# Attention values with 512 moving columns per matmul in a one-core hybrid decoder layer

## The chip, the cores and the metric

The kernel runs on one core of one Trainium2 chip. The metric is the device time of one execution in microseconds, the median of several runs. A profile of one more execution shows what each engine did and when. The engines named below are PE (TensorE, matmuls), PEld (its loading of stationary operands), ACT (ScalarE), DVE (VectorE), POOL (GpSimd) and SP (SyncE, which issues most transfers here).

## The reference

One decoder layer over 512 tokens of width 2048: a mixer whose two halves run side by side (stick-breaking attention with 8 heads of 128, and a gated linear recurrence), then an MLP of width 8192. Both sub-layers are preceded by a norm whose shift and scale come from a conditioning vector `c`. Cut to what matters here:

```python
mod = (c_act @ w_ada[l] + b_ada[l]).reshape(B, N_MOD, D)
sh1, sc1, gt1, sh2, sc2, gt2 = [mod[:, j][:, None, :] for j in range(N_MOD)]

h = rmsnorm(x, g_norm_mix[l]) * (1.0 + sc1) + sh1
proj = jnp.einsum('bsd,de->bse', h, w_in[l])
q, k, v, xr, xg = jnp.split(proj, ...)          # widths 1024 each

o_attn = stick_breaking_attention(to_heads(q), to_heads(k), to_heads(v))
...
y = jnp.einsum('bse,ed->bsd', mixed, w_out[l])
x = x + gt1 * y
h = rmsnorm(x, g_norm_mlp[l]) * (1.0 + sc2) + sh2
hid = jnp.square(jax.nn.relu(jnp.einsum('bsd,df->bsf', h, w_mlp_in[l])))
x = x + gt2 * jnp.einsum('bsf,fd->bsd', hid, w_mlp_out[l])
return rmsnorm(x, g_norm_final)
```

The change concerns `v`, the attention values: `h` (512 tokens x 2048) times a 2048 x 1024 part of `w_in`.

## The kernel before, in words

All activations are kept transposed, feature by token, in 16 blocks of 128 features (`k` from 0 to 15); a block of all 512 tokens is one tile of 128 x 512. Products are computed to nearly full float32 precision by three matmuls: each operand is split into a high part, rounded to the format that PE streams quickly (`F32R`), and a low part, the rest. High x high, high x low and low x high are added up in one PSUM bank.

A matmul has a stationary operand (128 x 128, loaded by PEld) and a moving operand (128 partitions by up to 512 columns), and writes 128 x columns into PSUM. The groups of the profile name the moving operand first: `ps_mm<-a,wh` has a moving `a` tile and a stationary slice of a `wh` tile.

For queries, keys and all later products (`mm3`, L258) the weights are stationary and the 512 tokens move. For the values (`v_mm`, L463) it is the other way about, because attention needs them token by feature: the stationary operand is a block of 128 tokens of `hT[k]` (tiles with the tag `a`), and the weights move (tiles `wh` and `wl`, each 128 x 512, the values' weights of four heads for one `k`). The four banks that a group of values uses are filled over all 16 `k`; then `v_evac` (L474) has ACT copy each bank to a high part and DVE subtract it for the low part, and `vt` records where the values of each head and token block lie.

The stages around the change, in order of time:

- L416: the recurrence's input product over all `k`, with the first half of the modulation rows made beside it.
- L489: for each `k`, queries and keys of heads 0 and 1 (four banks `mm`, twelve matmuls), then values of heads 0 to 3 (banks `z` and `o`). `prep2` (L386) makes `hT[k + 2]` beside it on DVE and ACT, with a modulation row.
- `qk_group(2)` (L746): queries and keys of heads 2 and 3, with the attention of heads 0 and 1 woven in.
- `v_group(4)` (L750): values of heads 4 to 7 in four banks `mm`, with the attention of heads 2 and 3 (`scores`, `shares`, `values`) and modulation rows (`adas`, L696, whose passes over `w_ada` are L211) woven in. Its last two `k` are done bank by bank in `ending` (L305), so that each bank is evacuated as it is finished.
- `qk_group(4)` and `qk_group(6)`, with the gates of the recurrence (L569, moving tiles `x`) and attention, the gate branch, the output product, and from L1080 the MLP by Strassen's scheme in steps of 256 columns (L1099 to L1101).

What is woven in comes in `Lane`s (L269): generators whose pieces are written into the program between the main matmuls at a set pace (`tick`). The whole program is then put into an order for each engine by a list scheduler, which takes the ready instruction of the highest priority, judged by its own model of times. Priority is the position in the program; `tc.high_priority(offset=n)` moves it `n` instructions ahead. Weights (`weights`, L230: a transfer on SP into `wr`, a high part by ACT into `wh`, a low part by DVE into `wl`) have an offset of `URGENT` = 150, evacuations one of `EVAC` = 88. There are four `wr` and three each of `wh` and `wl`.

Of the kernel before, what the change touches and what calls it, by code (L numbers as in the profile page):

```python
# [12 lines left out]
AF = mybir.ActivationFunctionType  # L13
ALU = mybir.AluOpType
PSUM = bass.MemoryType.PSUM

P = 128
S = 512
D = 2048
NK = D // P  # L20
# [44 lines left out]
def hybrid_layer_kernel(  # L65
# [32 lines left out]
    def T(tag, dt=F32, cols=None):  # L98
        return new(next(split_tag) if tag == "w4" else tag, dt, cols)
# [13 lines left out]
    act = nc.scalar.activation  # L113
    stt = nc.vector.scalar_tensor_tensor
    tt = nc.vector.tensor_tensor
    mm = nc.tensor.matmul

    def f32(ap):
        return ap.bitcast(F32)
# [110 lines left out]
    def weights(src, tag=None, urgent=URGENT, pin=False):  # L230

        n = src.shape[-1] if len(src.shape) == 2 else src.shape[1] * src.shape[2]
        with tc.high_priority(offset=urgent):
            r = T("wr" if tag not in ("w3", "w4", "ts") else "raw")
            dst = r[:, :n] if len(src.shape) == 2 else r[:, :n].rearrange("p (a b) -> p a b", b=src.shape[2])
            dma = nc.sync.dma_start(dst, src)
            if pin:
                later(dma)
            if tag in ("w4", "ts"):
                both = T(tag, F32R)  # L240
                h, lo = both[:, :S], both[:, S : 2 * S]
            else:
                h, lo = T(tag or "wh", F32R), T(tag or "wl", F32R)
            act(h[:, :n], r[:, :n], AF.Copy)  # L244
            low(lo[:, :n], r[:, :n], h[:, :n])
        return h, lo
# [18 lines left out]
    def blk(o):  # L265
        return slice(o * P, (o + 1) * P)
# [100 lines left out]
    xs, xhl, hT = {}, {}, {}  # L367
# [35 lines left out]
    def weights1(k, halves=(0, 1)):  # L403
        return [weights(w_in[blk(k), XR + i * 512 : XR + (i + 1) * 512], tag="a", urgent=min(k * 28, URGENT), pin=True) for i in halves]
# [6 lines left out]
    w = weights1(0, [0])  # L411
# [4 lines left out]
    for k in range(NK):  # L416
# [18 lines left out]
        for hf in range(2):  # L435
            wh, wl = w[hf]
            for o in range(4):
                mm3(banks[hf * 4 + o], wh[:, blk(o)], wl[:, blk(o)], *xhl[k], k == 0, k == NK - 1)
        w = w_next
    xr_t = []  # L440
    for o in range(8):
        t = T("a")
# [5 lines left out]
    qk, vt, o_t = {}, {}, []  # L448
# [13 lines left out]

    def v_mm(bs, w, k, os=range(4)):  # L463

        ah, al = hT[k]
        for o, b in ((o, b) for o in os for b in (o % 2 * 2, o % 2 * 2 + 1)):
            wh, wl = (t[:, o // 2 * 256 : o // 2 * 256 + 256] for t in w)
            out = bs[o][:, (b % 2) * 256 : (b % 2) * 256 + 256]
            st = k == 0 and b % 2 == 0
            mm(out, ah[:, blk(b)], wh, start=st, stop=False, skip_group_check=True)  # L470
            mm(out, al[:, blk(b)], wh, start=False, stop=False, skip_group_check=True)
            mm(out, ah[:, blk(b)], wl, start=False, stop=k == NK - 1, skip_group_check=True)

    def v_evac(bs, h0, os=range(4)):  # L474

        for o in os:
            p, b = o // 2, o % 2
            h, lo = T("a", F32R), T("a", F32R)
            with tc.high_priority(offset=EVAC):
                act(h, bs[o], AF.Copy)  # L480
                tt(out=lo, in0=bs[o], in1=f32(h), op=ALU.subtract)
            for j in range(2):
                for hd in range(2):
                    c = slice(j * 256 + hd * P, j * 256 + (hd + 1) * P)
                    vt[(h0 + 2 * p + hd, 2 * b + j)] = (h[:, c], lo[:, c])


    banks = [bank(t) for t in BANKS]
    for k in range(NK):  # L489
        if k + 2 < NK:  # L490
            prep2(k + 2)
        wh, wl = weights(src_qk[blk(k), :, : 2 * P])
        for o in range(4):
            mm3(banks[o], wh[:, blk(o)], wl[:, blk(o)], *hT[k], k == 0, k == NK - 1)
        v_mm(banks[4:], weights(src_v(k, 0, 4)), k)
    qk_evac(banks[:4], 0)
    v_evac(banks[4:], 0)

    def qk_group(h0, begun=(0, None)):
# [3 lines left out]
    def v_group(h0):  # L503
        bs = [bank("mm") for _ in range(4)]
        load, step = lambda k: weights(src_v(k, h0, 4)), lambda k, w, os: v_mm(bs, w, k, os)
        for k in range(NK - 2):
            step(k, load(k), range(4))
            tick()
        ending(load, step, range(NK - 2, NK), lambda o: v_evac(bs, h0, [o]))
# [308 lines left out]
    def out_evac(outs, g, tok, held=None):  # L818
# [35 lines left out]
        out=gm2, in0=mods[:, SC2 * NK : (SC2 + 1) * NK], scalar=1.0, in1=vec[:, C_GMLP : C_GMLP + NK],  # L854
# [225 lines left out]
    def strassen(src, acts, after=None, pre=None, before=None, js=range(8)):  # L1080

        bs = [bank(next(turn)) for _ in PRODUCTS]
        if pre:
            n, ts = pre
            with tc.high_priority(offset=SETE):
                for b, t in zip(bs, ts):
                    act(b, t, AF.Copy)
                for b, t in zip(bs[5:], load_pre(n, (5, 6), nc.scalar)):
                    act(b, t, AF.Copy)
        if before:  # L1090
            loaded[0] = before()
        for j in js:
            w, a = operands(src(j)), acts(j)
            for b, (an, wn) in zip(bs, PRODUCTS):
                (ah, al), (wh, wl) = a[an], w[wn]
                for i in range(2):
                    out, st = b[:, q_(i)], j == js[0] and i == 0 and not pre
                    kw = dict(skip_group_check=True)
                    mm(out, wh[:, blk(i)], ah, start=st, stop=False, **kw)  # L1099
                    mm(out, wh[:, blk(i)], al, start=False, stop=False, **kw)  # L1100
                    mm(out, wl[:, blk(i)], ah, start=False, stop=j == js[-1], **kw)  # L1101
            if after:
                after(j)
            tick()
        return bs
# [108 lines left out]
    for g in range(1, NG):  # L1214
# [3 lines left out]
        bs = strassen(lambda j: w_pair[j][:, :, g * 512 : (g + 1) * 512], acts_in, last, js=range(KP)[:: -1 if g == 1 else 1])  # L1218
# [29 lines left out]
    for i, (n, ps) in enumerate(parts):  # L1248
# [11 lines left out]
        bs = strassen(src, acts_out, after, nxt, before, ps)  # L1260
        nxt = loaded[0]
        if n not in left and n < NO - 1:
# [10 lines left out]
            with tc.high_priority(offset=SETW):  # L1273
                for k, tok, q in quarters(n, *qs):
                    t = x2[k][:, tok]
# [8 lines left out]
        else:  # L1284
            with tc.high_priority(offset=SETE):
                for j, b in enumerate(bs):
                    t = T("a")
# [14 lines left out]
    for p in final:  # L1302
        t = T("a", F32R)
# [156 lines left out]
```

## Time and profile before

| | |
|---|---|
| time, median of 3 runs | 2004.98 us (2004.24 to 2006.26) |
| time of the profiled execution | 2004.49 us |
| its span, first to last instruction | 2002.8 us |
| instructions in the profile | 37929 |
| PE: busy, matmuls | 1947.9 us (97%), 14532 |
| DVE: busy | 1761.3 us (88%) |
| ACT: busy | 1076.5 us (54%) |
| granted TensorE clock, mean | 0.995 |
| HBM read and written | 375.25 MB and 63.70 MB |
| matmuls of L470, L471, L472 | 256 each, 128x256 |
| DVE passes over `w_ada` rows, L211 | 160 of 128x1024, about 1.22 us each |

Busy times are sums over the span, and PE's are of overlapping matmuls whose ends the profiler models; a matmul of 256 columns is shown with some 0.28 us but the next one starts 0.11 to 0.12 us later. Where PE works without a pause, the distance from one start to the next is the cost, and it is read from the timeline. A row of the timeline has start, duration, engine, line, operation, output<-inputs, shape and count; where an engine had been idle before, brackets give how long and what ended it. A row of the waits has the engine and line that waited, what it waited for, microseconds in total, times and the longest.

### The profile page before, as it was taken

What the parts mean: (1) busy time and instruction counts of PE and PEld (TensorE: products, weight loads), DVE (VectorE), ACT (ScalarE), POOL (GpSimd) and SP (SyncE); (2) the same over time, 40 slices, a digit from 0 to 9 for tenths busy, and PEclk for the clock granted to TensorE, in tenths of its full rate; (3) what the DMA queues carried; (4) which work ended last, traced back from release to release, by engine and by line L of the source; (5) the groups of instructions that cost most, each with busy time, mean ns of one, the idle gap of its engine ahead of it and who ended that gap; (6) DMA issues with size and microseconds to landing.
All of it is one profiled execution on the core that took longest, in us unless ns stands there. A gap on an engine that the chain in (4) does not pass through costs nothing. (4 is left out here: it accounts for less than half of the span.)

```text
span 2002.8 us, 37929 instructions
## 1 busy us (share of the span) xinstructions
PE 1947.9 (97%) x14532; PEld 1837.3 (92%) x14532; DVE 1761.3 (88%) x2971; ACT 1076.5 (54%) x1572; POOL 181.2 (9%) x283
## 2 busy tenths in 40 slices
PE   8999999999999998999999999999999999999997
PEld 6789898788888898999999999999999999999996
DVE  8998786878998599999999999999879879788986
ACT  4443564786533385555555556556445545555542
POOL 0000000000000000112111211200110210210000
PEclk9999999999999999999999999999999999999998
DMA  9896655556779544766666666755577667677644
GB/s 364 303 318 215 207 167 184 181 150 215 226 250 369 170 139 138 233 196 213 217 193 208 227 195 193 228 177 195 185 250 252 247 246 273 229 254 272 235 148 153
DMA packets 205624, 441.45 MB, mean 220 GB/s; under 512 B 20353, under 2 KB 41985, under 8 KB 205442
## 3 DMA queue, kind: packets, MB, share of 16 engines
q1 hardware_dynamic: 178642, 360.78, 54.9%
q0 software_dynamic: 21760, 71.32, 9.5%
q10 hardware_dynamic: 5040, 6.93, 1.0%
q8 instruction: 114, 1.87, 0.4%
q14 instruction: 68, 0.56, 0.1%
HBM read 375.25 MB, written 63.70 MB: 219 GB/s over the span
## 5 line engine op out<-in xcount | busy, mean ns | idle before, releaser
L1099 PE MATMUL ps_mm<-a,w 128*128 128x256 f32 x1696 | 468.8, 277 | 2.3 <-DVE a L1111 1.2
L1101 PE MATMUL ps_mm<-a,w 128*128 128x256 f32 x1696 | 468.9, 277 | 2.1 <-DVE w L122 1.9
L1100 PE MATMUL ps_mm<-a,w 128*128 128x256 f32 x1696 | 468.8, 277 | 0.3 <-DVE a L122 0.3
L1069 ACT ACTIVATE w<-ts 128x1024 fp32r<-128x1024 f32 x244 | 258.8, 1061 | 273.9 <-DVE ts L1065 248.7
L1101 PE MATMUL ps_z<-a,w 128*128 128x256 f32 x1304 | 361.6, 278 | 8.3 <-DVE w L122 8.3
L1099 PE MATMUL ps_z<-a,w 128*128 128x256 f32 x1304 | 361.5, 278 | 3.6 <-DVE a L1115 1.6
L1100 PE MATMUL ps_z<-a,w 128*128 128x256 f32 x1304 | 361.1, 277 | 0.1
L122 DVE TENSOR_TENSOR w<-ts,w 128x1024 fp32r<-128x1024 f32 x244 | 298.6, 1224 | 58.6 <-PE ps_mm L1101 26.5
L1099 PEld LDWEIGHTS ps_mm<-a,w 128*128 128x128 f32 x1696 | 318.6, 188 | 3.6 <-issue 2.5
L1101 PEld LDWEIGHTS ps_mm<-a,w 128*128 128x128 f32 x1696 | 318.9, 188 | 2.9 <-DVE w L122 2.8
L1100 PEld LDWEIGHTS ps_mm<-a,w 128*128 128x128 f32 x1696 | 319.0, 188 | 0.7 <-DVE a L122 0.7
L122 DVE TENSOR_TENSOR w<-raw,w 128x768 fp32r<-128x768 f32 (+1 forms) x296 | 268.5, 909 | 39.0 <-ACT w L244 23.6
L1063 ACT ACTIVATE w<-raw 128x768 fp32r<-128x768 f32 x244 | 204.8, 840 | 169.8 <-issue 85.5
L1101 PEld LDWEIGHTS ps_z<-a,w 128*128 128x128 f32 x1304 | 245.4, 188 | 10.0 <-DVE w L122 9.9
L1099 PEld LDWEIGHTS ps_z<-a,w 128*128 128x128 f32 x1304 | 245.7, 188 | 5.0 <-issue 2.1
L1100 PEld LDWEIGHTS ps_z<-a,w 128*128 128x128 f32 x1304 | 245.8, 189 | 0.6 <-DVE a L122 0.6
L244 ACT ACTIVATE wh<-wr 128x512 fp32r<-128x512 f32 (+1 forms) x184 | 113.4, 620 | 152.3 <-PE ps_mm L262 65.2
L259 PE MATMUL ps_mm<-a,wh 128*128 128x512 f32 x448 | 176.2, 393 | 3.7 <-DVE a L460 1.6
L1057 DVE TENSOR_TENSOR ts<-raw 128x512 f32<-128x512 f32 x244 | 167.8, 688 | 12.8 <-DMA raw<-in_w_mlp_out_dram 11.9
L263 PE MATMUL ps_mm<-a,wl 128*128 128x512 f32 x448 | 175.1, 391 | 0.4 <-DVE wl L122 0.2
L262 PE MATMUL ps_mm<-a,wh 128*128 128x512 f32 x448 | 174.8, 390 | 0.0
L122 DVE TENSOR_TENSOR wl<-wr,wh 128x512 fp32r<-128x512 f32 (+1 forms) x184 | 124.7, 681 | 33.3 <-ACT wh L244 32.5
(332 smaller groups left out, 4154.4 us busy)
## 6 DMA issues: line engine op xcount, KB each, us to landing
raw<-in_w_mlp_out_dram SPq DMA_DIRECT2D x124, 512.0 KB, 4.2
raw<-in_w_mlp_in_dram SPq DMA_DIRECT2D x120, 512.0 KB, 3.9
x<-in_w_adaT_dram SPq DMA_DIRECT2D x108, 512.0 KB, 5.8
wr<-in_w_in_dram SPq DMA_DIRECT2D x160, 256.0 KB, 3.4
tt<-in_w_adaT_dram SPq DMA_DIRECT2D x52, 512.0 KB, 6.5
part<-a POOLq DMA_DIRECT2D x84, 256.0 KB, 3.9
a<-part SPq DMA_DIRECT2D x84, 256.0 KB, 6.4
prod<-a POOLq DMA_DIRECT2D x63, 256.0 KB, 5.8
```

What stands on the lines that cost most here:

```text
L122: tt(out=out, in0=full, in1=f32(high), op=ALU.subtract)
L244: act(h[:, :n], r[:, :n], AF.Copy)
L259: first = mm(out, wh, ah, start=start, stop=False, **kw)
L262: mm(out, wh, al, start=False, stop=False, **kw)
L263: mm(out, wl, ah, start=False, stop=stop, **kw)
L1057: tt(out=t[:, : 2 * HT].rearrange("p (a b) -> p a b", a=2), in0=r[:, HT : 3 * HT].rearrange("p (a b) -> p a b", a=2), in1=r[:, q_(0)].unsq ...
L1063: act(h, r[:, HT:], AF.Copy)
L1069: act(h, t, AF.Copy)
L1099: mm(out, wh[:, blk(i)], ah, start=st, stop=False, **kw)
L1100: mm(out, wh[:, blk(i)], al, start=False, stop=False, **kw)
L1101: mm(out, wl[:, blk(i)], ah, start=False, stop=j == js[-1], **kw)
```

## The change

For each `k`, the values' products no longer go through pairs of heads (256 moving columns) but through all four heads at once (512 moving columns), past the same token blocks. A bank used to hold two token blocks of two heads, side by side in its halves; it now holds one token block of four heads. The count of matmuls, and of loads of stationary operands, goes from 24 to 12 for each `k`. The order of the three products, the tiles, the banks, the transfers and the evacuations' shapes are as before; `vt` points to other slices.

```diff
     def v_mm(bs, w, k, os=range(4)):
 
-        ah, al = hT[k]
-        for o, b in ((o, b) for o in os for b in (o % 2 * 2, o % 2 * 2 + 1)):
-            wh, wl = (t[:, o // 2 * 256 : o // 2 * 256 + 256] for t in w)
-            out = bs[o][:, (b % 2) * 256 : (b % 2) * 256 + 256]
-            st = k == 0 and b % 2 == 0
-            mm(out, ah[:, blk(b)], wh, start=st, stop=False, skip_group_check=True)
-            mm(out, al[:, blk(b)], wh, start=False, stop=False, skip_group_check=True)
-            mm(out, ah[:, blk(b)], wl, start=False, stop=k == NK - 1, skip_group_check=True)
+        (ah, al), (wh, wl) = hT[k], w
+        for b in os:
+            mm(bs[b], ah[:, blk(b)], wh, start=k == 0, stop=False)
+            mm(bs[b], al[:, blk(b)], wh, start=False, stop=False)
+            mm(bs[b], ah[:, blk(b)], wl, start=False, stop=k == NK - 1)
 
     def v_evac(bs, h0, os=range(4)):
 
-        for o in os:
-            p, b = o // 2, o % 2
+        for b in os:
             h, lo = T("a", F32R), T("a", F32R)
             with tc.high_priority(offset=EVAC):
-                act(h, bs[o], AF.Copy)
-                tt(out=lo, in0=bs[o], in1=f32(h), op=ALU.subtract)
-            for j in range(2):
-                for hd in range(2):
-                    c = slice(j * 256 + hd * P, j * 256 + (hd + 1) * P)
-                    vt[(h0 + 2 * p + hd, 2 * b + j)] = (h[:, c], lo[:, c])
+                act(h, bs[b], AF.Copy)
+                tt(out=lo, in0=bs[b], in1=f32(h), op=ALU.subtract)
+            for hd in range(4):
+                vt[(h0 + hd, b)] = (h[:, blk(hd)], lo[:, blk(hd)])
```

## The prediction

> **What bounds the kernel now.** I read the page first, then the busy times by stretches, then the waits of the two stretches in which the change lies, then the timeline of single matmuls there. The page says which engine to look at:
>
> ```profile
> PE 1947.9 (97%) x14532; PEld 1837.3 (92%) x14532; DVE 1761.3 (88%) x2971; ACT 1076.5 (54%) x1572; POOL 181.2 (9%) x283
> ```
>
> PE is busy for 97% of the span, but an average doesn't say what a stage is worth. `v_mm` runs in two: in the loop of L489, beside the first query and key products (about 104 to 198 us), and in `v_group(4)` (about 256 to 318 us). The busy times of these stretches, in the order PE, PEld, DVE, ACT, POOL, then granted clock, DMA share and GB/s:
>
> ```profile
> 104.00:198.00 94.00, 94.00 (x594) 85.45 (x593) 84.91 (x150) 36.64 (x61) 0.00 (x0) 1.00 0.79 268
> 256.00:318.00 62.00, 61.67 (x483) 60.34 (x482) 45.43 (x79) 35.23 (x52) 0.00 (x0) 1.00 0.54 170
> ```
>
> PE has no idle time in the first and 0.33 us in the second, at full clock. DVE is nearly as full in the first (84.91 of 94), so it has to be excluded as the real bound. The waits do that. PE waits for nothing in the first stretch and has one row in the second; ACT, which makes the high parts of the weights, waits for PE:
>
> ```profile
> PE ps_mm L470 <- DVE a L460: 0.3, 1, 0.3
> ```
>
> ```profile
> ACT wh L244 <- PE ps_o L471: 14.2, 8, 2.3
> ```
>
> The next weights are held up until PE gives a buffer back: PE is the late one, and a faster PE gets its weights earlier. So in both places the time is the sum of the steps from one matmul's start to the next one's, and the question is what a step costs in the old form and in the new.
>
> The timeline gives the steps (start, duration, line, form):
>
> ```profile
> 110.72 0.28 PE L470 MATMUL ps_z<-wh,a 128*128 128x256 f32 x1
> ...
> 113.47 0.28 PE L472 MATMUL ps_o<-wl,a 128*128 128x256 f32 x1
> 113.59 0.40 PE L259 MATMUL ps_mm<-a,wh 128*128 128x512 f32 x1
> ...
> 114.98 0.39 PE L259 MATMUL ps_mm<-a,wh 128*128 128x512 f32 x1
> ...
> 116.34 0.28 PE L470 MATMUL ps_z<-wh,a 128*128 128x256 f32 x1
> ```
>
> From 110.72 to 113.59 lie the 24 value matmuls of one `k`: 2.87 us, 0.120 each. From 113.59 to 116.34 lie 12 query and key matmuls with 512 columns: 2.75 us; the last six, from 114.98, take 1.36, or 0.2267 each, the first six 1.39. The value matmuls run at 0.120 in `v_group` too, five steps in 0.60:
>
> ```profile
> 258.02 0.28 PE L470 MATMUL ps_mm<-wh,a 128*128 128x256 f32 x1
> ...
> 258.62 0.28 PE L472 MATMUL ps_mm<-wl,a 128*128 128x256 f32 x1
> ```
>
> **The change, part by part.** The groups by line and form count what is replaced:
>
> ```profile
> L470 PE MATMUL ps_mm<-wh,a 128*128 128x256 f32 x128 | 36.5, 285 | 0.3 <-DVE a L460 0.3
> L470 PE MATMUL ps_z<-wh,a 128*128 128x256 f32 x96 | 27.1, 282 | 0.0
> L470 PE MATMUL ps_o<-wh,a 128*128 128x256 f32 x32 | 9.1, 283 | 0.0
> ```
>
> That is 256 matmuls of L470, as many of L471 and L472: 768 of 256 columns, 24 for each of 32 `k`. After the change there are 384 of 512 columns, 12 for each `k`, with half as many weight loads. The columns streamed are the same number. A gain can come only from a cost per matmul, or per load, that does not grow with columns. Is there one? Strassen's 256-column matmuls say no:
>
> ```profile
> 967.75 0.28 PE L1099 MATMUL ps_o<-a,w 128*128 128x256 f32 x1
> ...
> 969.00 0.28 PE L1101 MATMUL ps_z<-a,w 128*128 128x256 f32 x1
> ```
>
> Eleven steps in 1.25 us are 0.1136 each, half of the settled 0.2267 within the rounding. There, halving the count would save nothing. The value matmuls pay 0.120, about 6.5 ns more. The means by form show who else pays:
>
> ```profile
> L1100 PE MATMUL ps_mm<-a,w 128*128 128x256 f32 x1696 | 468.8, 277 | 0.3 <-DVE a L122 0.3
> L471 PE MATMUL ps_mm<-wh,a 128*128 128x256 f32 x128 | 36.2, 283 | 0.0
> L262 PE MATMUL ps_z<-a,wh 128*128 128x512 f32 x96 | 37.3, 389 | 0.0
> L262 PE MATMUL ps_z<-x,wh 128*128 128x512 f32 x16 | 6.3, 395 | 0.0
> L262 PE MATMUL ps_o<-tt,a 128*128 128x512 f32 x8 | 3.2, 394 | 0.0
> ```
>
> A name list reads moving operand first. Where an `a` tile streams, the means are 277 and 389 ns. Where a `wh`, `x` or `tt` tile streams, they are 283, 395 and 394: 5 or 6 ns more, at 256 columns and at 512 alike. The steps agree, as six gate matmuls of 512 columns show, which stream `x`:
>
> ```profile
> 342.21 0.39 PE L259 MATMUL ps_z<-x,wh 128*128 128x512 f32 x1
> ...
> 343.61 0.39 PE L259 MATMUL ps_mm<-a,wh 128*128 128x512 f32 x1
> ```
>
> 1.40/6 is 0.2333, again 6.6 ns above 0.2267. So I read the surcharge as about 6.6 ns for each matmul whose moving operand is not an `a` tile, whatever its length. Why, the trace doesn't say. The new matmuls still stream `wh` and `wl`; the nearest row, `values`, even has their pairing, a stationary `a` tile under another tile's stream.
>
> The sum: a new block of values takes 12 x 0.2333 = 2.80 us. In the first loop it replaces 2.87: 0.07 for each of 16 `k`, 1.1 us. In `v_group` it replaces 24 x 0.120 = 2.88: 0.08 x 16 = 1.3 us. Together **2.4 us**. The query and key matmuls that follow stay: their 0.03 of slower first steps (1.39 against 1.36) also stand behind the gates, from 343.61 on.
>
> The unknown is the step of a 512-column matmul that streams `wh`, and it is bounded from both sides. At 0.2267 the block takes 2.72; the first loop saves 0.15 and at most the 0.03 behind it, `v_group` 0.16: (0.18 + 0.16) x 16 = 5.4 us. At 0.240, twice the old step, nothing is saved. I take 0.2333, since both 512-column forms that stream another tile (395 and 394) point to it.
>
> The Trainium skill, page "TensorE: Matmul & The Clock Gate", section "Back-to-back issue gap", has a warm step of N/2.4 + 2.5 ns, which is a fixed 2.5 ns per matmul; by it the change would save 384 x 2.5 ns, an estimate of 1.0 us. The trace disagrees on both sides: 0.1136 against 0.2267 leaves no room for a fixed part where an `a` tile streams, and 6.6 ns is more than 2.5 where it doesn't.
>
> The other parts cost nothing I can find. The evacuations (`v_evac`) stay eight pairs of a 512-wide ACT copy and a DVE subtraction, on the same banks in the same order; only what a bank holds changes, one token block for four heads in place of two blocks for two heads. `values` of a head then needs four banks rather than two, but it comes several ticks into the next group. An evacuation is freed by a matmul 0.11 longer (0.39 against 0.28), once per group's end. No DMA, no wait and no buffer is added. The priorities (`URGENT`, `EVAC`) count instructions, and 150 now reach further ahead, but weights are capped by their three `wh` buffers, as the waits of ACT on PE show. What the planner does with half as many matmuls in its queue may still shuffle DVE's order: that is the rival on the slow side.
>
> After the two stages PE stays the busiest engine, and transfers and DVE work follow its progress, so I let the 2.4 us pass to the end. The profiled execution took 2004.49 us, 1.7 outside its span of 2002.8; its sum is 2002.1. The median of the runs is 2004.98, half a microsecond above that execution, and I forecast against it: 2002.6.
>
> **The rivals.** *The pace of weight loads.* PE loads 128 stationary columns per matmul, and where matmuls are narrower the loads set the step:
>
> ```profile
> 261.38 0.19 PEld L263 LDWEIGHTS ps_z<-a,a 128*128 128x128 f32 x1
> 261.49 0.19 PEld L259 LDWEIGHTS ps_z<-a,a 128*128 128x128 f32 x1
> ```
>
> They start 0.11 apart, just under the 0.120 of the value matmuls. If 0.120 is a load's pace there, 512 columns hide it, the step is 0.2267 and the whole 5.4 us come: **1999.6**. For it: PE's steps are no wider than loads are. Against: gates and `values` pay 6.6 ns at 512 columns, where loads have slack. The same page of the Trainium skill, section "LDWEIGHTS (loading the stationary operand)", gives 128/1.2 = 107 ns; the 0.11 agrees, and it lies under 0.120.
>
> *The surcharge grows with columns.* Then 0.240 each, and the change makes fewer instructions and no time: **2005.0**. Against it are the same two rows at 512.
>
> *Slower: the entry to `qk_group(4)`.* PE's steps there, and DVE's and SP's queues just before:
>
> ```profile
> 317.79 0.39 PE L259 MATMUL ps_mm<-a,wh 128*128 128x512 f32 x1
> 318.59 0.50 PE L263 MATMUL ps_mm<-a,wl 128*128 128x512 f32 x1 [0.19 <-DVE wl L122]
> 319.88 0.47 PE L259 MATMUL ps_mm<-a,wh 128*128 128x512 f32 x1 [0.56 <-DVE a L481]
> 320.19 0.39 PE L262 MATMUL ps_mm<-a,wh 128*128 128x512 f32 x1
> ```
>
> ```profile
> 316.70 1.23 DVE L211 SCALAR_TENSOR_TENSOR x<-x,cb 128x1024 f32<-128x1024 f32 x1 [0.28 <-DMA x<-in_w_adaT_dram]
> 317.85 1.29 DVE L122 TENSOR_TENSOR wl<-wr,wh 128x512 fp32r<-128x512 f32 x2
> 319.05 1.28 DVE L481 TENSOR_TENSOR a<-ps_mm,a 128x512 fp32r<-128x512 f32 x2
> ```
>
> ```profile
> 310.61 0.94 SPq L199 DMA_DIRECT2D x<-in_w_adaT_dram  x2
> ```
>
> Five steps take 2.40 us where 5 x 0.227 = 1.14 would do: 1.3 lost, because a pass over a modulation row (L211), itself late by its transfer, stands in DVE's queue ahead of the low parts and the last evacuations. PE will come here earlier. If the planner puts more passes ahead, each costs 1.23 and its 0.08 of accumulator reading, 1.3 us; two eat the gain, and four, two such issues of SP, leave 5.2 - 2.4 = 2.8 us: **2007.8**. Five at this place, or the same at the next groups' entries, pass 0.2%. For it: DVE's order is made from counts that change. Against: PE coming early makes low parts no later, and their priority is higher than a row's.
>
> **How the numbers follow.** Forecast 0.52, load pace 0.22, surcharge by columns 0.13, slower entry 0.13. The 2.5 ns of the page would fall among the third's. A measurement of this kernel can tell some 0.2%, 4.0 us, from no change, so even a right forecast is most likely read as the same. Faster by more: most of the load pace (0.19) and a fifth of the forecast, where a stall downstream falls away by luck (0.10), 0.29 in all. Slower by more: half of the slow entry and a little of the rest, 0.09. Same: 0.62. The range runs from 1999.3, the load pace's end, to 2006.4, half way into the slow entry, with a tenth left out on each side; the forecast's own case spans 2001.5 to 2004.
>
> **What will show it.** The three lines of `v_mm` should have 128 matmuls each, of 512 columns, with means of 394 or 395 ns (389 is the load pace's sign, and about 400 with steps of 0.240 the columns'). One `k` of the first loop should take 5.55 us instead of 5.62, the gates' steps should stay at 0.2333. PE should lose about 1.3 us at the entry to `qk_group(4)`; more than 3.7 there means that the slow rival won. I am wrong if the steps are as forecast but the end moves by another amount: then stalls after 318 us were reshuffled.

## The result: the steps gained more than forecast, and the end came later

| | before | after |
|---|---|---|
| median of the runs on one chip | 2004.94 us (2002.15 to 2008.62, 13 runs) | 2010.77 us (2006.25 to 2016.1, 13 runs) |
| ratio to before | | 1.0031, 95% interval 1.0021 to 1.004 |
| profiled execution, its span | 2004.49, 2002.8 us | 2015.17, 2013.4 us |

The changed kernel is slower by 0.3%, which lies above the range of the prediction. Its profiled execution is one of its longer ones, 4.4 us above the median, so the balance of the two traces (10.6 us between the spans) overstates the loss of the median (5.8 us).

The page of the changed kernel, first the line of busy times:

```profile
PE 1949.6 (97%) x14148; PEld 1822.9 (91%) x14148; DVE 1761.0 (87%) x2971; ACT 1073.5 (53%) x1570; POOL 181.2 (9%) x283
```

There are 384 matmuls fewer, as the change says, and PE's share is the same 97%. The groups by line and form (the lines of `v_mm` are now L467 to L469; everything behind `v_evac` has moved up by 6 lines):

```profile
L259 PE MATMUL ps_mm<-a,wh 128*128 128x512 f32 x448 | 177.1, 395 | 8.5 <-DVE a L460 7.4 <-ACT wh L244 0.5 <-DVE a L477 0.2
...
L468 PE MATMUL ps_mm<-wh,a 128*128 128x512 f32 x64 | 25.0, 390 | 0.0
...
L468 PE MATMUL ps_z<-wh,a 128*128 128x512 f32 x48 | 18.7, 389 | 0.0
...
L468 PE MATMUL ps_o<-wh,a 128*128 128x512 f32 x16 | 6.2, 389 | 0.0
```

The new matmuls stand at 389 and 390 ns, not at 394 or 395: that is the sign that the prediction gave to the rival of the load pace. (The 64 of L467 in `v_group`, not shown, have a mean of 396 but a median of 389, since a few of them start behind a wait.) The first row already shows where the time went: query and key matmuls had PE idle for 7.4 us until an evacuation (L460). One `k` of the first loop in the timeline:

```profile
108.87 0.39 PE L467 MATMUL ps_z<-wh,a 128*128 128x512 f32 x1
...
111.59 0.39 PE L259 MATMUL ps_mm<-a,wh 128*128 128x512 f32 x1
...
114.31 0.39 PE L467 MATMUL ps_z<-wh,a 128*128 128x512 f32 x1
```

Twelve value matmuls take 111.59 - 108.87 = 2.72 us, 0.2267 each, and a whole `k` 5.44 us where it was 5.62: 0.18 x 16 = 2.9 us in this loop, over twice the 1.1 that was forecast for it. So the steps of the change did get faster. Three stretches of the changed kernel, in the same view as in the prediction:

```profile
104.00:198.00 94.00, 93.79 (x417) 77.56 (x417) 86.24 (x153) 38.83 (x64) 0.00 (x0) 1.00 0.78 269
256.00:318.00 62.00, 59.63 (x289) 50.08 (x289) 46.14 (x80) 32.14 (x46) 0.00 (x0) 0.99 0.58 178
420.00:470.00 50.00, 40.77 (x177) 32.99 (x176) 36.25 (x62) 34.69 (x52) 0.00 (x0) 0.91 0.54 164
```

The third stretch of the changed kernel isn't one in which the change lies. The same stretch of the kernel before, in the same view:

```profile
420.00:470.00 50.00, 47.91 (x228) 39.27 (x227) 41.47 (x73) 43.39 (x63) 0.00 (x0) 1.00 0.60 185
```

PE had 47.91 us of work in it and now has 40.77, and the mean granted clock fell from 1.00 to 0.91. To see where the two kernels part, I took the start of the same piece of work in each trace. The first column is the kernel before, in microseconds; the others are the differences from it, for the changed kernel and for five of the experiments that follow (whose columns are explained there):

```
                                          before   after  halves   banks  pinned    mix  mirror
first values into bank o, first loop      112.87   -1.96   -0.42   -1.03   +1.22  +0.20   -1.08
last values of the first loop             197.65   -4.91   -3.38   +0.03   +1.22  -2.76   -4.03
shares of head 3 begin                    297.32   -3.78   -3.09   -0.01   +1.89  -4.52   -3.77
shares of head 4 begin                    388.83   -2.12   -2.52   +1.88   +2.77  -5.04   -2.74
shares of head 5 begin                    409.52   -0.71   -2.51   +1.89   +4.18  -5.02   -1.33
shares of head 6 begin                    453.97   +7.71   -3.36  +10.67  +12.53  -5.87   +6.99
shares of head 7 begin                    475.58   +9.70   -3.36  +12.51  +14.81  -5.87   +9.09
first Strassen matmul                     762.61  +10.14   -1.81  +11.79  +14.99  -6.85   +9.28
last matmul                              1990.45  +10.60   -4.74  +10.72  +12.13  -9.69   +6.57
```

The changed kernel is 4.91 us ahead after the first loop (1.96 of which it had before the loop's first `k` was done; the other columns show that the start differs by a microsecond or two from one execution to the next), by head 5 has given nearly all of its lead back, and between heads 5 and 6 falls behind by 7.71 + 0.71 = 8.4 us, with 2.0 more before head 7. Then little changes. (The first row of "banks" isn't a head start: its order of matmuls reaches bank `o` nine matmuls earlier.) **So nearly the whole net loss is made at one place, and what PE waits for there** stands in the waits from 420 to 470 us of the changed kernel (PE's row and one of ACT's):

```profile
PE ps_mm L259 <- DVE a L460: 6.6, 2, 6.4
...
ACT a L459 <- DVE a L589: 1.1, 1, 1.1
```

and of the kernel before, from 420 to 490 us:

```profile
PE ps_mm L259 <- DVE a L460: 0.8, 1, 0.8
PE ps_z L652 <- DVE tt L122: 0.8, 1, 0.8
PE ps_z L652 <- ACT tt L642: 0.5, 1, 0.5
```

PE waits for the last bank of `qk_group(6)` to be evacuated. L459 is ACT's copy of the high part, L460 DVE's subtraction. ACT's timeline in the changed kernel:

```profile
439.74 2.17 ACT L584 ACTIVATE x<-x 128x512 f32<-128x512 f32 x4
441.93 1.28 ACT L1405 ACT_TABLE_LOAD   x1
444.35 0.60 ACT L459 ACTIVATE a<-ps_mm 128x512 fp32r<-128x512 f32 x1 [1.13 <-DVE a L589]
```

DVE's there:

```profile
443.04 2.34 DVE L589 TENSOR_TENSOR_SCAN a<-a,a 128x512 f32<-128x512 f32 x2
445.29 0.67 DVE L587 TENSOR_TENSOR a<-x,a 128x512 f32<-128x512 f32 x1
445.87 0.69 DVE L460 SCALAR_TENSOR_TENSOR a<-ps_mm,a 128x512 fp32r<-128x512 f32 x1
```

And PE's:

```profile
439.80 0.39 PE L263 MATMUL ps_mm<-a,wl 128*128 128x512 f32 x1
446.61 0.79 PE L259 MATMUL ps_mm<-a,wh 128*128 128x512 f32 x1 [6.43 <-DVE a L460]
```

In the kernel before, the same copy ran at 435.21, with no wait:

```profile
434.21 0.59 ACT L459 ACTIVATE a<-ps_mm 128x512 fp32r<-128x512 f32 x1
...
435.21 0.59 ACT L459 ACTIVATE a<-ps_mm 128x512 fp32r<-128x512 f32 x1
```

Why should a copy out of PSUM wait for the scan of the recurrence (L589), with which it shares no data? Because it shares a buffer. ACT writes into a new `a` tile; there are 64 of them for the whole kernel, and a new one takes the place of an old one that nobody will read again. The programs name the semaphores on which these four copies wait, in their order (first the kernel before, then the changed one):

```
L459 ACTIVATE a_4320<-ps_mm_3764 128x512 [waits PE_49]
L459 ACTIVATE a_4336<-ps_mm_3765 128x512 [waits PE_49]
L459 ACTIVATE a_4367<-ps_mm_3766 128x512 [waits PE_49]
L459 ACTIVATE a_4381<-ps_mm_3767 128x512 [waits PE_49]

L459 ACTIVATE a_3936<-ps_mm_3380 128x512 [waits PE_49]
L459 ACTIVATE a_3952<-ps_mm_3381 128x512 [waits PE_49]
L459 ACTIVATE a_3983<-ps_mm_3382 128x512 [waits PE_49]
L459 ACTIVATE a_3997<-ps_mm_3383 128x512 [waits DVE_49,PE_49]
```

By the addresses in the two programs, the last of them takes, in the kernel before, the place of a value tile of heads 4 and 5 (last read by `values(5)`, which ends inside `qk_group(6)`), and in the changed one that of a recurrence tile, last read by the scan. A value tile used to hold two heads, and the four tiles of heads 4 and 5 came free two heads early. Now every tile holds all four heads, and none comes free before `values(7)`, in the next group. When the copy takes its tile, 61 of the 64 are in use before and 63 after. The scheduler also put the copy behind the square roots (L584) and the table load, as ACT's timeline shows.

Where the lead went before head 5 is a second question, and the traces answer it only in part. With the gain of `v_group`, some 6.7 us were lost between 193 and 409 us. PE waited 0.9 us at 210 and 1.4 at 254 to 257. And at two places the granted clock was at half, which leaves 1.7 us of 3.4 unused; the kernel before, whose rows stand first, had the full clock there:

```profile
317.20:320.60 3.40, 2.65 (x11) 1.00 0.27 78
388.90:392.20 3.30, 3.10 (x21) 1.00 0.70 228
...
317.20:320.60 3.40, 3.40 (x10) 0.50 0.87 243
388.90:392.20 3.30, 3.30 (x13) 0.50 0.54 184
```

Each half clock follows a pause of PE of 1.3 or 1.4 us. The second shows as the 1.41 us that three columns of the table (after, pinned, mirror) lose alike between heads 4 and 5. The kernel before and "halves", "banks" and "mix" have the same pause there and keep the full clock, so the tile lives aren't shown to be its cause; what decides is open.

### The profile page after: what moved, and what is told of

Same layout as the page of the kernel before. It is cut to its first block, busy times and chain, and to the rows that moved or that the text cites. A ratio compares the mean times of both kernels' runs of the same rounds, so it can differ in the third digit from the quotient of the medians.

```text
span 2013.4 us, 37157 instructions
## 1 busy us (share of the span) xinstructions
PE 1949.6 (97%) x14148; PEld 1822.9 (91%) x14148; DVE 1761.0 (87%) x2971; ACT 1073.5 (53%) x1570; POOL 181.2 (9%) x283
## 5 line engine op out<-in xcount | busy, mean ns | idle before, releaser
L122 DVE TENSOR_TENSOR w<-ts,w 128x1024 fp32r<-128x1024 f32 x244 | 298.5, 1223 | 61.3 <-PE ps_mm L1095 28.6
L122 DVE TENSOR_TENSOR w<-raw,w 128x768 fp32r<-128x768 f32 (+1 forms) x296 | 268.4, 908 | 39.3 <-ACT w L244 23.3
L211 DVE SCALAR_TENSOR_TENSOR x<-x,cb 128x1024 f32<-128x1024 f32 x108 | 131.9, 1225 | 26.3 <-DMA x<-in_w_adaT_dram 26.3
```

Of the source, the lines that this page charges most:

```text
L122: tt(out=out, in0=full, in1=f32(high), op=ALU.subtract)
L211: ins = stt(out=t, in0=t, scalar=1.0, in1=cb[q_], op0=ALU.mult, op1=ALU.mult, accum_out=self.ga[:, q_ : q_ + 1],)
```

## The experiments

The theory was the **tile lives**: the 512-column matmuls gain their 5.4 us, and the stall comes only from which heads share a tile. Its rivals: that wider matmuls, with fewer instructions, let the scheduler reorder the queues to worse effect, whatever the tiles; and, for the steps, that the 0.120 us of the old matmuls was something other than a load's pace.

**512 columns, with tiles for two heads ("halves").** The matmuls and banks of the changed kernel; each bank is evacuated in two halves, and two banks' halves of the same two heads fill one tile.

```diff
         for b in os:
-            h, lo = T("a", F32R), T("a", F32R)
-            with tc.high_priority(offset=EVAC):
-                act(h, bs[b], AF.Copy)
-                tt(out=lo, in0=bs[b], in1=f32(h), op=ALU.subtract)
-            for hd in range(4):
-                vt[(h0 + hd, b)] = (h[:, blk(hd)], lo[:, blk(hd)])
+            for p in range(2):
+                if b % 2 == 0:
+                    v_pair[(h0, p, b // 2)] = T("a", F32R), T("a", F32R)
+                h, lo = v_pair[(h0, p, b // 2)]
+                src, at = bs[b][:, p * 256 : p * 256 + 256], slice(b % 2 * 256, b % 2 * 256 + 256)
+                with tc.high_priority(offset=EVAC):
+                    act(h[:, at], src, AF.Copy)
+                    tt(out=lo[:, at], in0=src, in1=f32(h[:, at]), op=ALU.subtract)
...
```

> 512-column value matmuls as in the changed kernel, but each bank is evacuated in two halves of 256 columns, into tiles that hold one pair of heads and two token blocks, as the tiles of the kernel before did: the four tiles of heads 4 and 5 are free again after the values of head 5. Eight evacuations of 512 columns become sixteen of 256 in each of the two stages. Theory (lifetime: the changed kernel loses its time because the value tiles of heads 4 and 5 live until head 7 is done, so that the last evacuation of the queries and keys of heads 6 and 7 waits for a tile of the recurrence): that evacuation waits for no scan, PE's idle time of 6.6 us at 440 us is gone, the steps stay at 0.227, and the time is some 5 us under the kernel before, 1999 to 2002. Rival (the planner's order, shuffled by half as many matmuls in its count): the idle time stays or comes back elsewhere, 2008 to 2012.

Measured: 2000.38 us (1995.93 to 2005.9, 12 runs) beside 2002.54 of the kernel before on that chip, ratio 0.9982 (0.9971 to 0.9992). PE's waits from 420 to 490 us:

```profile
PE ps_z L652 <- DVE tt L122: 0.8, 1, 0.8
PE ps_z L652 <- ACT tt L642: 0.5, 1, 0.5
```

The wait for L460 is gone, with the wide matmuls in place. So the wide matmuls don't make the stall. The gain is smaller than 5.4 us: 2.2 by the medians. The waits from 190 to 215 us show one piece of it, a wait which neither the kernel before nor the changed one has there:

```profile
PE ps_z L259 <- DVE a L481: 1.3, 2, 0.8
```

L481 is DVE's part of the evacuation by halves, eight subtractions of 256 columns instead of four of 512 where the first loop ends.

**256 columns, with tiles for four heads ("banks").** The reverse: the changed kernel's banks, tiles and evacuation, filled by the old matmuls with 256 columns.

```diff
-        for b in os:
-            mm(bs[b], ah[:, blk(b)], wh, start=k == 0, stop=False)
...
+        for p, b in ((p, b) for p in range(2) for b in os):
+            v = slice(p * 256, p * 256 + 256)
+            out = bs[b][:, v]
+            mm(out, ah[:, blk(b)], wh[:, v], start=k == 0 and p == 0, stop=False, skip_group_check=True)
...
```

> The banks and tiles of the changed kernel (one token block of four heads), filled by the 256-column matmuls of the kernel before: 768 matmuls again, half a bank each. Theory (lifetime): the value steps are 0.120 as before and the wait for the scan at the last evacuation before the gate branch is there, so it is slower than the changed kernel by its 5 us of steps: 2014 to 2018, 10 to 13 us above the kernel before. Rival (planner's order by counts): the counts are those of the kernel before, so 2004 to 2006.

Measured: 2016.66 us (2011.66 to 2019.33, 4 runs), ratio 1.0058 (1.0041 to 1.0076). PE's waits from 420 to 490 us:

```profile
PE ps_mm L259 <- DVE a L460: 6.6, 1, 6.6
PE ps_z L648 <- DVE tt L122: 2.3, 1, 2.3
```

The same 6.6 us without a single wide matmul, and no gain to set against it: the table's column is at 0.03 after the first loop and at -0.01 at head 3, and ends at 10.72. The stall belongs to the new banks and tiles, not to the width of the matmuls.

**The kernel before, its tiles kept longer.** The last test of the theory changes neither matmuls nor banks nor tiles: behind `values(7)` four one-column copies on DVE read the tiles of heads 4 and 5, so that these live as long as in the changed kernel. The copies went into a small tile of their own.

```diff
+    scrap = const(4, "scrap")
...
+        if h0 == 6:
+            for i, part in enumerate(vt[(4, 0)] + vt[(4, 2)]):
+                later(nc.vector.tensor_copy(scrap[:, i : i + 1], f32(part)[:, :1]))
```

> The kernel before, with four copies of one column on DVE after the values of head 7, which read the value tiles of heads 4 and 5 and so keep them until then; matmuls, banks and evacuations are those of the kernel before. Theory (lifetime): the last evacuation before the gate branch waits for the scan, PE idles 6 to 7 us at about 443 us, and the time is 10 to 13 us above the kernel before, 2014 to 2018. Rival (planner's order by counts, or the banks' layout): the four copies cost under 0.5 us, 2004 to 2006.

Measured: 2037.47 us (2035.59 to 2040.17, 4 runs), ratio 1.0162 (1.0146 to 1.0178). The stall was there (PE waited 5.8 us for the evacuation in one piece), but the loss was three times too large: 14 us behind at head 7, and another 22 us by the end, nearly all of it in the Strassen stage, whose steps had grown. The copies had brought one thing more than a longer life: a new tile, which moved every tile allocated behind it on that side of the memory by 32 bytes. That was to be told apart, so the copies went into a tile that exists already ("pinned"):

```diff
-    const(PAD, "pad")
+    scrap = const(PAD, "pad")
```

> The kernel before with the same four one-column copies as the run before it of this kind, now written into columns of the existing tile `pad`, so that no tile is added and no address moves. If the length of the value tiles' lives is what costs, and the other 24 us of the earlier run came from the moved addresses: the stall of the key and query groups comes back at 440 to 470 us (near 6 and 3 us), the late stage is as in the kernel before, and the time is 10 to 13 us above it (2012 to 2016 beside 2002.5). If the copies themselves or the long lives cost in the late stage too: 30 us or more above it again.

Measured: 2013.08 us (2009.54 to 2016.63, 6 runs) beside 2003.39, ratio 1.0041 (1.0028 to 1.0054): 9.7 us more, where the theory had 10 to 13. PE's waits from 420 to 490 us:

```profile
PE ps_mm L259 <- DVE a L460: 6.6, 2, 6.0
PE ps_z L652 <- DVE tt L122: 2.9, 1, 2.9
```

Four copies of one column, with nothing else changed, cost the kernel before 9.7 us; the whole change cost it 5.8 with 5.4 of faster steps to set against that. The programs agree with the waits: in the kernel before, in "halves" and in "mix" (below) the last copy takes the place of a value tile, with 61 tiles in use; in the changed kernel, "banks", "pinned" and the mirror it takes that of a recurrence tile last read by the scan, with 63. The tile lives are shown as the cause of the stall from both sides.

**Which of the two places?** Tiles for four heads in the first loop and tiles for two heads, by halves, in `v_group(4)` ("mix"), and the mirror image of it. Both have 512 columns everywhere; one condition in `v_evac` decides (`h0 == 4` in the mirror):

```diff
+            if h0 == 0:
+                h, lo = T("a", F32R), T("a", F32R)
+                with tc.high_priority(offset=EVAC):
+                    act(h, bs[b], AF.Copy)
...
```

> The 512-column matmuls in both places; heads 0 to 3 evacuated bank by bank into tiles of four heads, as in the changed kernel, and heads 4 to 7 into tiles of two heads by half banks. If only the long lives of the value tiles of heads 4 to 7 cost, the stall at 440 us is gone and the time is that of the kernel with tiles of two heads in both places or 1 us less, since 8 evacuations fewer stand at the entry to the first key and query group: 1999 to 2001. If the long lives of heads 0 to 3 cost as well: stalls of 1 us or more between 250 and 320 us and 2002 to 2006.

> The mirror image of the run before: 512-column matmuls in both places, heads 0 to 3 evacuated into tiles of two heads by half banks, heads 4 to 7 bank by bank into tiles of four heads, as in the changed kernel. If the long lives of the value tiles of heads 4 to 7 alone make the stall: PE waits near 440 us for 5 to 7 us and near 465 us for 2 to 3 us again, and the time is that of the changed kernel or up to 4 us below it (2003 to 2009). If both places have to live long for it: no such stall, and 1995 to 2001.

Measured: the mix 1995.14 us (1994.81 to 1998.04, 5 runs) beside 2003.39, ratio 0.9958 (0.9946 to 0.9971); the mirror 2009.31 us (2005.03 to 2021.68, 10 runs) beside 2004.88, ratio 1.002 (0.9998 to 1.0042). PE's waits from 420 to 490 us, the mix:

```profile
PE ps_z L660 <- DVE tt L122: 0.8, 1, 0.8
PE ps_z L660 <- ACT tt L650: 0.6, 1, 0.6
```

and the mirror:

```profile
PE ps_mm L259 <- DVE a L460: 6.8, 1, 6.8
PE ps_z L660 <- DVE tt L122: 2.7, 1, 2.7
```

The stall follows the tiles of heads 4 to 7, at the sizes expected; the mix is 4 us faster than expected, and the mirror 0.3 us above its range. For the stall only those tiles matter. The mix is faster than the kernel before and than the changed one. Its column in the table is the gain without the loss: -2.76 - 0.20 = -2.96 us in the first loop, and from -2.57 (shares of head 1, just before `v_group(4)`) to -5.04 (shares of head 4) another 2.5. Together 5.4 us, the sum of the load-pace rival to a tenth. The rest, to -9.69, came later; those are waits that fell differently, 2.8 us of them in the Strassen stage, and I have not traced them to the change.

**What the old step of 0.120 us was made of.** The products of one block of tokens reordered, so that two matmuls in a row use the same stationary operand (`ah` under `wh`, then `ah` under `wl`):

```diff
-            mm(out, al[:, blk(b)], wh, start=False, stop=False, skip_group_check=True)
-            mm(out, ah[:, blk(b)], wl, start=False, stop=k == NK - 1, skip_group_check=True)
+            mm(out, ah[:, blk(b)], wl, start=False, stop=False, skip_group_check=True)
+            mm(out, al[:, blk(b)], wh, start=False, stop=k == NK - 1, skip_group_check=True)
```

> The kernel before with the three products of the values in the order high x high, high x low, low x high, so that two of three matmuls in a row have the same stationary block. Theory A (0.120 is the pace of loading a new stationary block under this stream): loads are issued for each matmul all the same, the steps stay at 0.120 and the time at 2004 to 2006. Theory B (a load of the block that is already there is faster, which is why Strassen's steps are 0.1136): the steps fall to 0.113 to 0.118 and the time by 1.5 to 5 us.

Measured: 2001.68 us (1999.04 to 2007.59, 10 runs) beside 2002.54, ratio 0.9994 (0.9983 to 1.0005). The timeline of its first `k`:

```profile
110.13 0.28 PE L470 MATMUL ps_z<-wh,a 128*128 128x256 f32 x1
...
113.00 0.40 PE L259 MATMUL ps_mm<-a,wh 128*128 128x512 f32 x1
```

Twenty-four matmuls in 2.87 us, 0.120 each, as before: an unchanged stationary operand saves nothing, and the trace still shows one load for each matmul (256 of L471 in this run). That fits the load's pace but doesn't prove it, since Strassen's matmuls, each with a load as well, step at 0.1136. What is settled is that the values' surcharge of 6.5 ns is not paid at 512 columns.

**The moved addresses.** The kernel before with the existing `pad` wider, first by 32 bytes and then by 64, and nothing else:

```diff
-PAD, SHIFT = 8, 16
+PAD, SHIFT = 16, 16
```

> The kernel before with the tile `pad` 16 columns wide instead of 8: nothing is computed otherwise, but all tiles allocated behind it on that side start 32 bytes further on. If that shift is what slowed the late 256-column matmuls in the run with the scrap tile: about 20 to 27 us slower than the kernel before, with those matmuls' steps longer than 0.1136 us and no stall at 440 us. If the shift is harmless: the time of the kernel before within 0.2%.

> The kernel before with the tile `pad` 24 columns wide instead of 8, so that the tiles behind it start 64 bytes further on, where a width of 16 put them 32 bytes further on. If it is the start within 64 bytes that slows the late matmuls: the time of the kernel before within 0.2%, late 256-column steps back at 0.113 to 0.114 us. If any move of the tiles slows them: about 20 us slower again.

Measured: 2026.9 us for 16 columns (2025.22 to 2028.26, 4 runs) beside 2003.39, ratio 1.0112 (1.0098 to 1.0126); 2022.08 us for 24 (2018.79 to 2028.24, 5 runs) beside 2004.88, ratio 1.0085 (1.0056 to 1.0113). The busy time of PE from 1500 to 1700 us, inside the Strassen stage, with the count of its matmuls: the kernel before, then with `pad` at 16 columns, at 24, with the new tile `scrap`, and with the pinned copies in `pad`:

```profile
1500.00:1700.00 200.00, 200.00 (x1767) 1.00 0.72 257
```

```profile
1500.00:1700.00 200.00, 200.00 (x1712) 1.00 0.74 267
```

```profile
1500.00:1700.00 200.00, 200.00 (x1719) 1.00 0.75 269
```

```profile
1500.00:1700.00 200.00, 200.00 (x1711) 1.00 0.75 269
```

```profile
1500.00:1700.00 200.00, 200.00 (x1768) 1.00 0.77 273
```

At full clock and with no idle time PE starts 1767 matmuls in 200 us, 0.1132 each, or 1712, 0.1168 each, by nothing but where the tiles lie: the programs of the three have the same instructions in the same order. The first of these runs explains the 22 us that the run with `scrap` lost behind the stall. The second one's first reading, that the start within 64 bytes matters, falls: a move by 64 bytes costs nearly as much. Which tiles, and which property of their addresses, stays open.

## Why the prediction was wrong, by its own steps

**What bounds the kernel.** Right: PE's steps decide in both stretches, and a faster step there is a gain of the same size there (2.96 and 2.5 us in the mix).

**The step of a new matmul, 0.2333 us.** Too long: 0.2267, the lower end of the bounds given, and the gain of the steps is 5.4 us where the forecast had 2.4. The error lay in the reading of the surcharge as one of all matmuls "whose moving operand is not an `a` tile". It was read from two forms that differ from the new one in other ways too. The new one streams `wh` and `wl` and pays nothing, while the gates, which stream `x`, still step at 0.2333 in the changed kernel:

```profile
340.10 0.39 PE L259 MATMUL ps_z<-x,wh 128*128 128x512 f32 x1
...
340.80 0.39 PE L259 MATMUL ps_z<-x,wh 128*128 128x512 f32 x1
```

(three steps in 0.70 us). A form that speaks against the reading stood in the trace of the kernel before: the matmuls of `scores` stream an `a` tile, past a stationary `a` tile, and step at 0.121 with 256 columns but at 0.227 with 512 (medians of 24 and of 168 steps), so a surcharge at 256 that is gone at 512 could have been read there. What the gates and `values` pay for stays open. Of the two rivals about the step, the one called the load's pace gave the right size, 5.4 us and 389 ns, but its mechanism stays unproven; the one that grows with columns is out. The rule of the Trainium skill (page "TensorE: Matmul & The Clock Gate", section "Back-to-back issue gap") with its fixed 2.5 ns per matmul, an estimate of 1.0 us for the change, is not what these runs show either.

**"The other parts cost nothing I can find."** This is the step that failed, and the one that turned the sign. The sentence behind it has the fact in hand: "`values` of a head then needs four banks rather than two". I asked when `values` comes, that is, whether it would have to wait for its inputs, and didn't ask when its inputs come free. Each tile of values now has four readers instead of two, and its buffer is held until the last. "No buffer is added", and "the tiles ... are as before" in the account of the change, were true of the count and wrong of the time for which each is held. The runs show in its place a wait of 6.4 us for the last evacuation of `qk_group(6)`, whose tile the scan has to give back first. The claim that nothing changes but "what a bank holds" would have needed a count of the `a` tiles in use at each evacuation: 61 of 64, with 2 more to come.

**The slow rival, the entry to `qk_group(4)`.** Its mechanism is there. DVE's queue in the changed kernel:

```profile
311.16 1.22 DVE L211 SCALAR_TENSOR_TENSOR x<-x,cb 128x1024 f32<-128x1024 f32 x1
...
313.26 1.23 DVE L211 SCALAR_TENSOR_TENSOR x<-x,cb 128x1024 f32<-128x1024 f32 x1
314.41 0.08 DVE L211 DVE_READ_ACCUMULATOR x<-x,cb 128x1 f32 x1
314.41 1.29 DVE L122 TENSOR_TENSOR wl<-wr,wh 128x512 fp32r<-128x512 f32 x2
```

PE is earlier than it was, a row's pass still stands ahead of the low part that it needs, and PE waits for that low part:

```profile
315.15 0.50 PE L263 MATMUL ps_mm<-a,wl 128*128 128x512 f32 x1 [1.29 <-DVE wl L122]
```

Then comes the half clock from 317.2 us. From the first query and key matmul behind the values (316.40 us before, 311.89 now) to the first gate matmul (342.21, 340.10) lie 108 steps in both kernels; at 0.2267 they take 24.48 us, so PE loses 1.3 us of these 25.81 before and 3.7 of 28.21 now. The prediction's sign for this rival was more than 3.7, so by the sign alone it stands at the mark. But the rival was one of passes that each cost 1.3 us, with 5.2 lost; here the waits cost 1.9 us and the half clock, which it didn't have, 1.7 or so. The 2.4 lost against the kernel before is part of the gain and not the sign of the result; the mix has a wait of 0.9 there and is still the fastest.

**What would make it wrong.** The prediction named stalls after 318 us that are reshuffled, and that is the place: 440 us. It had no mechanism for them, and 0.09 for slower by more than 0.2% was too little for a kernel in which nearly all of these buffers are in use.

The price of the stall has two terms. PE stood for 6.6 us more than a step. Then it ran at half pace, as the windows of the changed kernel show (PE's busy time, granted clock, DMA share, GB/s); the clock fell while PE still stood:

```profile
440.20:443.40 3.20, 0.00 (x0) 1.00 0.56 169
443.50:446.60 3.10, 0.00 (x0) 0.50 0.84 299
446.60:450.00 3.40, 3.39 (x9) 0.50 0.03 12
450.00:453.00 3.00, 3.00 (x17) 0.95 0.32 87
```

The nine matmuls that start from 446.61 on end their steps at 450.30, in 3.69 us; six of 512 columns and three of 384 (0.173 each in the kernel before, from 439.38 to 439.90 us) take 6 x 0.2267 + 3 x 0.173 = 1.88 at full clock. That is 1.8 more, so the stall costs the changed kernel 6.6 + 1.8 = 8.4 us. That the table falls by 8.4 between heads 5 and 6 as well is chance: the kernel before loses about 1 us at the same place, and six matmuls (1.4 us) that it runs behind head 6's mark stand ahead of it in the changed kernel. Those come back between heads 6 and 7, where the column still falls by 2.0: PE waited 2.6 us for a low part of the attention weights (L122), and a half clock followed (0.76 on the mean from 465 to 472 us).

## What to carry to other kernels

When a change regroups data in tiles, list for every tile its last reader before and after, and count the live tiles of the pool at each place where a new one is taken; with a full pool a longer life turns into a wait on an instruction that has nothing to do with the data. Shape of the matmul and grouping of the tile can be chosen apart: here wide matmuls with narrow tiles, where the pool is full, and wide tiles elsewhere gave the gain without the loss. A surcharge read from two forms of an instruction is not yet a rule for a third.

## What the runs showed of the hardware

- A pause of 6.4 us on PE halved its granted clock: 1.00 up to 443.4 us, 3.2 us after PE fell idle, then 0.50 for the rest of the pause and until 450.0, 3.4 us after PE went on. A stall of this length cost a quarter more than it shows as waiting (1.8 us on 6.6). The Trainium skill (page "TensorE: Matmul & The Clock Gate", section "Part 1: The HAM clock gate (the 'warmup' mystery)") has a half clock after an idle window of about 3.4 us and the full clock again after a busy one; the trace agrees for this pause.
- The shorter pauses aren't covered by that: a half clock of 3.4 us followed pauses of 1.3 and 1.4 us in the changed kernel (0.50 from 317.2 to 320.6 us and from 388.9 to 392.2), and the pause of 1.3 to 1.4 us just before the shares of head 4, the same in all seven traces of the table, is followed by one in three of them and by none in four.
- Steps of the Strassen stage's 256-column matmuls depend on where the tiles lie: 0.1132 or 0.1168 us in the same program, with tiles moved by 32 bytes, 23.5 us of the whole kernel. A run that adds even a small tile compares two things at once.
